# A hybrid decoder step on one core: the attention projection as Strassen products, input forms split at their due times, and the second projection's first units by token halves

## The chip, the cores and the metric

The kernel runs on one core of one Trainium2 chip. The metric is device time in microseconds. An engine is named by its short name: PE is TensorE (matmul), PEld its weight loads, DVE is VectorE, ACT is ScalarE, POOL is GpSimd, SP is SyncE, which issues nearly all transfers here.

## The reference

One layer of a decoder trunk, in float32, for a prompt of 2048 tokens of width 1024 and for 8 single-token samples. What matters for this change:

```python
h = _rmsnorm(x, norm_g) * (1.0 + scale) + shift
z = h @ w_in                                   # 1024 x 6656
q, k, v, ga, xr, gr, ma, mr = jnp.split(z, offs, axis=-1)
...
ya = o * jax.nn.silu(ga)                       # o: attention in a window of 128
xc, conv_new = _causal_conv(xr, conv_buf, w_conv, b_conv)
hs, h_last = _rglru(xc, h0, w_ra, b_ra, w_rx, b_rx, lam)
yr = hs * jax.nn.silu(gr)
merged = jax.nn.sigmoid(ma) * (ya @ w_pa) + jax.nn.sigmoid(mr) * (yr @ w_pr)
y = x + gate * (merged @ w_out)
```

## The kernel before

**Halves and slots.** The prompt is worked on in two halves of 1024 tokens (`s` = 0 and 1), one after the other; the samples ride with the second half. In each half attention comes first (`phase_kv`, `phase_attn`), then `stages` builds a list `seq` of matmul units in a fixed order: the gates of attention `ga`, the two merge gates `ma` and `mr`, the recurrence's inputs `xr` and `gr` (`rnn`), the attention projection `pa`, the recurrence's projection `pr` and the output `out`. Results pass from stage to stage through scratch tensors in HBM: `yad` is the gated attention output, `yrd` that of the recurrence, `tmad` and `tmd` the tanh of the merge gates, `t1d` the attention term of the merge, `mgd` the merged rows, `hd` the normalised input. Each holds 8 row blocks of 128 channels by 1024 tokens, in two column halves of 512 tokens (`chunk`).

**Exact float32 by three products.** An operand is split into a high part in fp32r (ACT casts it) and a low part (DVE subtracts the high part from the source): `split_to`. A product of two such operands is three matmuls: high by high, high by low, low by high.

**Units.** A `Plain` unit computes one block of 128 output channels for 1024 tokens in four calls of `mm`, one for each pair of a contraction half `h` and a token half `c`. A `Fast` unit computes two such blocks (256 channels) by Winograd's variant of Strassen's scheme: seven products instead of eight, each a call of `mm`, in the order of `PROD`. Its right operands are seven forms of the input: three plain quarters (`x11`, `x21`, `x22`) and four differences (`T1` to `T4`). Its left operands are weight quarters and four sums of them (`s1` to `s4`, on DVE). A call of `mm` in either kind is 12 matmuls of 128 x 512. In Fast the results of two PSUM banks are kept and added by `keep`, `add` and `last`.

**The order of everything else.** `Line` runs through `seq`. At step t it issues `mm` number t, then the events registered for t, in the order of their rank (`EVAC`, `SIDE`, `SPLIT`, `FORM`, `CHAIN`, `LATE`, `STORE`, `LOAD`). All engines keep program order, so an event's step fixes its place in its engine's queue. Weights are loaded 7 steps before their unit (`LOADS`) and split 2 steps before their product (`AHEAD`). The recurrence's elementwise chain (`chain`) starts 12 steps after its pair of units and goes on for 27 more. Loads and stores share the queue of SP (`ld` and `st`).

**The stages around the change.** `seq` starts with 18 steps (`m1`, `mr0`, `ga1`); then come `pair(ga2, ga3)`, and four times `rnn(p)` followed, but for the last, by `pair(ma, mr)`. So `rnn_end` is step 130, and the chain of `rnn(3)` runs on into the projection. `forms_of_h` builds the seven forms of the normalised input at the start of the line: differences on DVE and POOL, and splits in `first`, `second` and `third`, at steps t0, t0 + 1 and from t0 + 2 on, for four k with t0 = -1, 1, 3, 5. `pa` takes 8 Plain units (steps 130 to 162); its operand is the 16 quarters of `yad`, split over 10 steps before `rnn_end`. `pr` takes 8 Plain units (162 to 194), its last two interleaved; its operand is the 16 quarters of `yrd`. `phase_h`, in the first half, normalises and transposes the second half's rows, from `rnn_end + 4` on. Step 0 is the first after attention.

**Rings.** SBUF tiles come from two rings in order of release: 28 tiles of 4 KB a partition (`S`) and 35 of 2 KB (`Tt`). The seven forms of the input fill all 28 `S` tiles, and the last unit that reads a form frees it (`final`).

**The start.** Constants of the recurrence (`c4`, `ba2`, and the transposed states `RT`) are made after the first normalisation and before attention.

Of the kernel before, what the change touches and what calls it, by code (L numbers as in the profile page):

```python
# [21 lines left out]
P = 128  # L22
# [19 lines left out]
def tile_hybrid_step(ctx: ExitStack, tc: tile.TileContext, x_prompt, x_sample, cache_k, cache_v, state_conv,  # L42
# [191 lines left out]
    V.memset(q1, 0.25)  # L234

# [107 lines left out]
    for t in wgr + [hsF, yaF]:  # L343
# [8 lines left out]
                                     for t in ("yad", "tmad", "tmd", "sgd", "yrd", "t1d", "mgd"))  # L352
    Gd = dp.tile([P, D], F32, tag="Gd", name="Gd")
# [57 lines left out]
    def phase_h(line, t0):  # L411

        def group(g, t0):
            xts = []

            def load(i):
                xts.append(S([D]))
                r0 = 1024 + g * 512 + i * P
                ld.dma_start(xts[i], xp[r0:r0 + P, :])

            def turn(f):
                ps = PT()
                for i in range(4):
                    T_.transpose(ps[:, i * P:(i + 1) * P], xts[i][:, f * P:(f + 1) * P], ident)
                line.after(1, EVAC, lambda: h_evac(1, ps, 512, f, g * 512, None))
                if f == KT - 1:
                    free(*xts)

            for i in range(4):
                line.on(t0 + 2 * i, LOAD, lambda i=i: load(i))  # L430
                line.on(t0 + 4 + 2 * i, CHAIN, lambda i=i: rms_rows([xts[i][:, h * 512:(h + 1) * 512] for h in range(2)], P))
# [122 lines left out]
    def phase_attn(s, hT, sa, kT, vt, chunks, line):  # L554
# [250 lines left out]
        prefetch(3)  # L805
        pinned[0] = s == 1
# [8 lines left out]
        for i in range(N + 2):  # L815
# [292 lines left out]
    class Fast:  # L1108
# [3 lines left out]
        def __init__(self, line, F, src, evac, samples=None, base=None, late=False):  # L1112
            self.line, self.F, self.src, self.evac, self.samples = line, F, src, evac, samples
            self.base, self.late, self.early = base, late, 0
# [27 lines left out]
        def place(self, s):  # L1142
# [6 lines left out]
            for i, j in ((0, 0), (1, 0), (0, 1), (1, 1)) if late else ((0, 0), (1, 0), (1, 1), (0, 1)):  # L1149
                line.on(s[0] - (3 if late and j == 1 else LOADS + self.early), LOAD, lambda i=i, j=j: self.load(i, j))  # L1150
# [109 lines left out]
    def stages(s, hT, hT1=None, side=None):  # L1260
# [17 lines left out]
        def forms_of_h(k, t0):  # L1278
# [25 lines left out]
            def second():  # L1304
                split("T1", "x11")
                split("T3", "x12")
                free(x["x11"], x["x12"])

            def third():
                split("T4", "x21")  # L1310
                free(x["x21"])
# [4 lines left out]
            line.on(t0 + 1, FORM, second)  # L1316
            line.on(max(t0 + 2, 3), FORM, third)
# [319 lines left out]
        yax, yrx = xtiles(), xtiles()  # L1637
        quarters = [(4 * h + k, c) for h in range(2) for c in range(2) for k in range(4)]
# [3 lines left out]
        def load_pair_rows(w, c0):  # L1642
            wr = w[:, c0:c0 + P].rearrange("(G gg j d) c -> G gg d j c", G=2, gg=2, j=4)

            def load(t, h):
                for gg in range(2):
                    ld.dma_start(t[gg * 64:gg * 64 + 64], wr[h, gg])
            return load

        def pa(f):  # L1650
            tm = {}

            def load(c):
                tm[c] = Tt([512])
                ld.dma_start(tm[c], chunk(tmad, f, c))

            def evac(c, ps):
                V.scalar_tensor_tensor(tm[c], tm[c], 1.0, ps, op0=ALU.add, op1=ALU.mult)
                line.after(1, STORE, lambda: store(c))

            def store(c):
                st.dma_start(chunk(t1d, f, c), tm[c])
                free(tm[c])

            z, d = zS[:, f:f + 1, :], maS[:, f:f + 1, :]
            u = Plain(line, yax, load_pair_rows(w_proj_attn[0], f * P), evac,
                      sample(yaF, z, lambda: V.scalar_tensor_tensor(d, d, 1.0, z, op0=ALU.add, op1=ALU.mult)))
            t0 = len(seq)
            seq.extend((u, n) for n in range(4))
            for c in range(2):  # L1670
                line.on(t0 + c, LOAD, lambda c=c: load(c))
            return u

        for f in range(KT):
            u = pa(f)
        u.gone = set(u.order)
        pa_end = len(seq)
        for i, (k, c) in enumerate(quarters):
            load_split(yrd, yrx, k, c, pa_end - 8 + i // 2 if i < 8 else pa_end - 3 + (i - 8) // 2, 3)

        def pr(f):
# [21 lines left out]
            def done():  # L1703
# [4 lines left out]
                      ((0, 0), (1, 0), (0, 1), (1, 1)) if f >= KT - 2 else Plain.ORDER)  # L1708
            t0 = len(seq)
            if f < KT - 2:  # L1710
                seq.extend((u, n) for n in range(4))
            for c in range(2):
                line.on(t0 + (c - 1 if f < KT - 2 else 4 * c + f - KT), LOAD, lambda c=c: load(c))
            return u

        for f in range(KT):
            last_pr, u = u, pr(f)
        u.gone = set(u.order)
# [118 lines left out]
        if s == 0:  # L1837
# [6 lines left out]
            phase_h(line, rnn_end + 4)  # L1844
# [73 lines left out]
    def state_out():  # L1918
# [11 lines left out]
        free(co)  # L1930
        yield
# [128 lines left out]
    for f in range(KT + 2):  # L2060
# [24 lines left out]
        if f == 4:  # L2085
# [13 lines left out]
    ba2 = C([P, 16], tag="ba2")  # L2099
    V.tensor_scalar(ba2, VT[:, 72:88], 0.5, None, op0=ALU.mult)  # L2100

# [11 lines left out]

    lam = VT[:, 88:96]
    e8, s8, q8, r8 = (M([8]) for _ in range(4))
    A.activation(e8, lam, AF.Abs)
    A.activation(e8, e8, AF.Exp, scale=-1.0)
    V.tensor_scalar(s8, e8, 2.0, None, op0=ALU.add)
    V.reciprocal(s8, s8)
    V.tensor_tensor(s8, s8, e8, op=ALU.mult)  # L2120
    V.tensor_tensor(q8, s8, s8, op=ALU.mult)
    V.tensor_scalar(r8, q8, 1.0 / 17, 1.0 / 15, op0=ALU.mult, op1=ALU.add)
    for n in (13, 11, 9, 7, 5, 3, 1):
        V.tensor_tensor(r8, r8, q8, op=ALU.mult)
        V.tensor_scalar(r8, r8, 1.0 / n, None, op0=ALU.add)
    V.tensor_tensor(r8, r8, s8, op=ALU.mult)
    V.tensor_scalar(s8, lam, -1.0, 0.0, op0=ALU.mult, op1=ALU.max)
    c4 = C([P, 16], tag="c4")
    V.scalar_tensor_tensor(c4[:, 0:8], r8, 2.0, s8, op0=ALU.mult, op1=ALU.add)
    V.tensor_scalar(c4[:, 0:8], c4[:, 0:8], 4.0, None, op0=ALU.mult)  # L2130
    V.tensor_scalar(c4[:, 8:16], c4[:, 0:8], -1.0, None, op0=ALU.mult)


    rows = S([D])
    ld.dma_start(rows[0:24], state_conv[0].rearrange("b r d -> (b r) d"))
    ld.dma_start(rows[24:32], state_h[0])
    ps = PT()
    for k in range(KT):
        T_.transpose(ps[:, k * 32:(k + 1) * 32], rows[0:32, k * P:(k + 1) * P], ident[0:32, 0:32])
    RT = C([P, KT, 32], tag="RT")  # L2140
    V.tensor_copy(RT, ps[:, 0:256].rearrange("p (k c) -> p k c", c=32))
    free(rows)

    hT1, side = [], {}
    line = stages(0, hT, hT1, side)
    attn = phase_attn(0, hT, None, kT, vt, chunks, line)
# [38 lines left out]
```

## Time and profile before

| | |
|---|---|
| median of 3 runs | 1958.66 us (1957.88 to 1959.34) |
| the profiled execution | 1961.09 us, its span 1959.4 us |
| PE, PEld | busy 1915.1 us and 1568.8 us |
| DVE, ACT, POOL | busy 1376.9, 984.5 and 392.3 us |
| matmuls | 11504 |
| transfers | 286.61 MB |

All rows of the profile carry line 60, the helper that records every operation, so groups are told apart by tiles: `pg`, `pq` and `pt` are PSUM pools, `S`, `B`, `H` and `M` are SBUF rings and pools. Matmuls overlap in the pipeline, so the mean of single records is longer than the time from one to the next; the latter counts. A form like `128*128 128x512` is the loaded weight tile and the moving operand.

### The profile page before, as it was taken

The numbers are of one execution on the slowest core, as the hardware profiler recorded it, in microseconds if no ns is written. First come the engines' busy times: TensorE is split into PE (matmuls) and PEld (weight loads), VectorE is DVE, ScalarE is ACT, GpSimd is POOL, SyncE is SP. The second block draws the span as 40 slices with busy tenths as digits, with TensorE's granted clock in tenths as the row PEclk, the third lists the DMA queues.
The fourth block names the chain that finished last, engine by engine and source line by source line (L and its number), as shares of the span: only waits on it lengthen the run. The fifth ranks groups of instructions, "written<-read, shape, count | busy, mean of one in ns | idle before, by whom it ended". The sixth has DMA issues, their size and how long they took to land. (4 is left out here: it accounts for less than half of the span.)

```text
span 1959.4 us, 32369 instructions
## 1 busy us (share of the span) xinstructions
PE 1915.1 (98%) x11504; PEld 1568.8 (80%) x11504; DVE 1376.9 (70%) x2862; ACT 984.5 (50%) x2167; POOL 392.3 (20%) x476
## 2 busy tenths in 40 slices
PE   6899999999999999999999999999999999999999
PEld 4798987778888878887898898777787887777777
DVE  3557778557888876588834777867687879745965
ACT  4445655336675766423423566543575667532321
POOL 3213433000111113060012344400010201111600
PEclk9899999999999999999999999999999999999999
DMA  9521124662433567986721111454233334558673
GB/s 281 176 66 46 53 92 154 180 184 82 142 120 95 164 182 250 327 262 195 231 59 51 47 47 59 152 145 140 87 123 105 120 97 164 149 171 293 216 235 108
DMA packets 307686, 286.61 MB, mean 146 GB/s; under 512 B 57073, under 2 KB 224229, under 8 KB 307486
## 3 DMA queue, kind: packets, MB, share of 16 engines
q1 hardware_dynamic: 307398, 282.41, 45.9%
q0 software_dynamic: 128, 2.15, 0.3%
q8 instruction: 90, 1.47, 0.3%
q14 instruction: 70, 0.57, 0.1%
HBM read 200.69 MB, written 85.93 MB: 146 GB/s over the span
## 5 line engine op out<-in xcount | busy, mean ns | idle before, releaser
L60 PE MATMUL pg<-S,B 128*128 128x512 f32 (+1 forms) x4224 | 1002.1, 392 | 1.5 <-DVE B L60 1.5
L60 PEld LDWEIGHTS pg<-S,B 128*128 128x128 f32 (+1 forms) x4224 | 774.2, 188 | 184.1 <-issue 11.1
L60 DVE TENSOR_TENSOR B<-B,B 128x512 fp32r<-128x512 f32 (+1 forms) x732 | 546.0, 769 | 148.0 <-ACT B L60 137.3
L60 PE MATMUL pq<-S,B 128*128 128x512 f32 (+2 forms) x1920 | 413.1, 379 | 10.0 <-DVE B L60 9.8
L60 PEld LDWEIGHTS pq<-S,B 128*128 128x128 f32 (+1 forms) x1920 | 317.7, 188 | 88.7 <-DVE B L60 14.0
L60 POOL TENSOR_TENSOR B<-B,B 128x512 f32<-128x512 f32 x128 | 191.9, 1516 | 950.6 <-DVE B L60 583.0
L60 ACT CAST B<-B 128x512 fp32r<-128x512 f32 x468 | 279.9, 617 | 114.2 <-DVE B L60 73.7
L60 PE MATMUL pg<-B,S 128*128 128x256 f32 x1872 | 242.8, 285 | 0.0
L60 PEld LDWEIGHTS pg<-B,S 128*128 128x128 f32 x1872 | 227.7, 189 | 10.1 <-issue 9.4
L60 DVE TENSOR_TENSOR S<-B,S 128x512 fp32r<-128x512 f32 x184 | 140.0, 789 | 25.7 <-ACT S L60 25.4
L60 ACT CAST S<-B 128x512 fp32r<-128x512 f32 x184 | 109.1, 621 | 88.5 <-DVE B L60 33.8
L60 ACT ACTIVATE B<-B 128x512 f32<-128x512 f32 (+1 forms) x150 | 93.2, 630 | 118.8 <-DVE B L60 110.4
L60 ACT ACTIVATE B<-B,M 128x129 f32<-128x129 f32 x260 | 102.7, 396 | 91.7 <-DVE M L60 87.5
L60 DVE SCALAR_TENSOR_TENSOR B<-B,pg 128x512 f32<-128x512 f32 x78 | 53.2, 683 | 73.8 <-PE pg L60 58.8
L60 ACT COPY H<-pt 128x256 f32<-128x256 f32 (+1 forms) x55 | 18.5, 337 | 160.6 <-PE pt L60 160.6
L60 DVE TENSOR_TENSOR B<-pq,B 128x512 f32<-128x512 f32 x96 | 66.0, 687 | 43.8 <-PE pq L60 37.9
L60 ACT COPY B<-pg 128x512 f32<-128x512 f32 x80 | 46.8, 585 | 93.0 <-PE pg L60 84.8
L60 POOL TENSOR_TENSOR B<-B,M 128x512 f32<-128x512 f32 x64 | 67.0, 1068 | 104.7 <-DVE M L60 104.7
L60 POOL TENSOR_TENSOR M<-M,mhalf 128x8 f32<-128x8 f32 (+4 forms) x70 | 84.2, 1203 | 5.8
L60 ACT ACTIVATE B<-pg 128x512 f32<-128x512 f32 x76 | 45.2, 595 | 79.8 <-PE pg L60 78.7
L60 DVE SCALAR_TENSOR_TENSOR B<-B,VT,B 128x512 f32<-128x512 f32 x96 | 81.2, 846 | 2.3
L60 DVE SCALAR_TENSOR_TENSOR B<-B,B 128x512 f32<-128x512 f32 x106 | 72.1, 685 | 0.6 <-ACT B L60 0.3
(201 smaller groups left out, 1685.8 us busy)
## 6 DMA issues: line engine op xcount, KB each, us to landing
B<-in_w_in_dram SPq DMA_DIRECT2D x144, 256.0 KB
B<-in_w_in_dram SPq DMA_DIRECT2D x128, 128.0 KB
B<-yad SPq DMA_DIRECT2D x56, 256.0 KB
B<-hd SPq DMA_DIRECT2D x48, 256.0 KB
B<-in_w_out_dram SPq DMA_DIRECT2D x48, 256.0 KB
S<-in_w_ada_dram SPq DMA_DIRECT2D x32, 256.0 KB
S<-in_x_prompt_dram SPq DMA_DIRECT2D x16, 512.0 KB
hd<-B SPq DMA_DIRECT2D x32, 256.0 KB
```

The costliest lines, as they stand in the source:

```text
L60: ins = fn(*args, **kw)
```

## The change

**Attention's projection** becomes four Fast units in two interleaved pairs: 28 steps in place of 32 in each half. Its operand is the seven forms of `yad`. The four differences of each k are taken on POOL (`differences`), from quarters loaded back from `yad`, and stored in a new scratch tensor `yfd`, at steps given by hand; `form_y` loads each of the 28 forms and splits it, from `rnn_end - 9` to `rnn_end + 10`. One `(tanh + 1)` factor in four is applied by DVE with the product, as before; for the other three ACT adds 1 (`plus`) and POOL multiplies. These units load their weights 5 steps ahead.

**The order before it:** the recurrences come first, each followed by a pair, with `ga2` and `ga3` in the first two: `rnn(0)`, `pair(ga2, mr1)`, `rnn(1)`, `pair(ga3, mr2)`, `rnn(2)`, `pair(ma1, mr3)`, `rnn(3)`, `pair(ma2, ma3)`. `rnn_end` stays step 130.

**The input forms** T1, T3 and T4 are split at steps 5 to 8, 7 to 10 and 10 to 13. **`pr`** starts with two units interleaved by token halves, and its operand's quarters come token half 0 first. **`phase_h`** loads rows in halves into the other ring, starts 14 steps later and sets its two groups 9 steps apart. **The recurrence's constants** become `rnn_constants`: loads after attention's first prefetch, the rest in attention's first step. Small ones: the load of the small vectors one step later at the start, `sample_attn`'s last step at 66, `state_out` at `pa_end`.

```diff
@@ phase_h
-                xts.append(S([D]))
+                xts.append([Tt([512]) for _ in range(2)])
...
-            group(g, t0 + 12 * g)
+            group(g, t0 + 9 * g)
@@ phase_attn
         prefetch(3)
+        next(aside, None)
...
+            for _ in aside:
+                pass
             if i != N:
                 slot(3)
@@ forms_of_h
-            line.on(t0 + 1, FORM, second)
-            line.on(max(t0 + 2, 3), FORM, third)
+            for n, src, t in (("T1", "x11", 5), ("T3", "x12", 7), ("T4", "x21", 10)):
+                line.on(t + k, FORM, lambda n=n, src=src: last(n, src))
@@ the order
-        pair(attn_gate(2), attn_gate(3))
-        for p in range(4):
+        ma = [merge(OFF_MA, p, tmad, maS) for p in range(1, 4)]
+        mr = [merge(OFF_MR, p, tmd, mrS) for p in range(1, 4)]
+        ga_end = []
+        for p, ab in enumerate(((attn_gate(2), mr[0]), (attn_gate(3), mr[1]), (ma[0], mr[2]), (ma[1], ma[2]))):
             end = rnn(p)
-            if p < 3:
-                pair(merge(OFF_MA, p + 1, tmad, maS), merge(OFF_MR, p + 1, tmd, mrS))
+            pair(*ab)
+            ga_end.append(len(seq))
@@ the operand of pa
-        for i, (k, c) in enumerate(quarters):
-            load_split(yad, yax, k, c, rnn_end - 11 + 10 * i // 16, 3)
+        def differences(k, t):
...
+            def sub(a, b, o, n):
+                G_.tensor_tensor(x[o], x[a], x[b], op=ALU.subtract)
+                line.after(2, STORE, lambda: st.dma_start(yfd[s, n, k], x[o]))
...
+            line.on(t, LOAD, load)
+            line.on(t + 4, FORM, first)
+            line.on(t + 6, FORM, second)
+            line.on(t + 9, EVAC, lambda: free(*x.values()))
+        for k in range(4):
+            differences(k, ga_end[k // 2] + (12, 41, 26, 39)[k])
+        def form_y(n, k, t):
...
+            line.on(t - 3, LOAD, load)
+            line.on(t, FORM, split)
+        for i, (n, k) in enumerate([(n, k) for _, n, _ in PROD for k in range(4)]):
+            form_y(n, k, rnn_end - 9 + 18 * i // 25)
@@ pa
+            def plus(i, j):
+                A.activation(tm[i, j], tm[i, j], AF.Identity, bias=onec)
+            def evac(i, j, x, t):
+                y = tm[i, j]
+                if t is None:
+                    V.scalar_tensor_tensor(y, y, 1.0, x, op0=ALU.add, op1=ALU.mult)
+                else:
+                    G_.tensor_tensor(y, y, x, op=ALU.mult)
+                    free(t)
+                line.after(1 if t is None else 2, STORE, lambda: store(i, j))
...
+        for p in range(0, 4, 2):
+            (a, la), (b, lb) = pa(p), pa(p + 1)
+            a.ahead = b.ahead = 5
+            t0 = pair(a, b)
@@ pr
-            load_split(yrd, yrx, k, c, pa_end - 8 + i // 2 if i < 8 else pa_end - 3 + (i - 8) // 2, 3)
+            load_split(yrd, yrx, k, c, pa_end - 9 + 7 * i // 8, 3)
...
+            if f == 1:
+                for n in (0, 2):
+                    seq.extend([(last_pr, n), (last_pr, n + 1), (u, n), (u, n + 1)])
@@ stages, at the end
-            phase_h(line, rnn_end + 4)
+            phase_h(line, rnn_end + 18)
...
-            line.steps(sample_attn(), range(7, 30), SIDE)
-            line.steps(state_out(), [end + 1], SIDE)
+            line.steps(sample_attn(), list(range(7, 27)) + [66], SIDE)
+            line.steps(state_out(), [pa_end], SIDE)
@@ the start
-        if f == 4:
+        if f == 5:
             next(rest)
```

More of the change, by code (lines that the diff above doesn't have):

```diff
@@ L234, in tile_hybrid_step @@
     V.memset(q1, 0.25)
+    onec = C([P, 1], tag="onec")
+    V.memset(onec, 1.0)
     def rstd_of(dst, ss, n, inv):
@@ L1302, in first, with last @@
                 free(x["x22"], x["T2"])
[L1304 to L1311, printed above, removed]
+            def last(n, src):
+                split(n, src)
+                free(x[src])
             line.on(t0 - 4, LOAD, load)
@@ L1650, in pa @@
[L1650 to L1672, printed above, removed]
@@ L2112, in tile_hybrid_step @@
     wk, wv = wkv[0][0] + wkv[1][0], wkv[0][1] + wkv[1][1]
[L2114 to L2142, printed above, removed]
     hT1, side = [], {}
     line = stages(0, hT, hT1, side)
-    attn = phase_attn(0, hT, None, kT, vt, chunks, line)
+    attn = phase_attn(0, hT, None, kT, vt, chunks, line, rnn_constants())
     pend = phase_kv(0, hT, None, kT, vt, wk, wv, list(enumerate(kvp)), range(4, 8), bias_expand(), attn)
```

120 lines of the change are left out of this document (96 added, 24 removed).

## The prediction

> **What bounds the kernel now.** First the page, for the engine that never rests; then the waits of TensorE and its instructions by shape; then the chain of waits, for the length of a group of matmuls; last the timeline and the windows around the places that the diff touches.
>
> ```profile
> span 1959.4 us, 32369 instructions
> PE 1915.1 (98%) x11504; PEld 1568.8 (80%) x11504; DVE 1376.9 (70%) x2862; ACT 984.5 (50%) x2167; POOL 392.3 (20%) x476
> L60 PE MATMUL pg<-S,B 128*128 128x512 f32 x4032 | 974.2, 397 | 1.5 <-DVE B L60 1.5
> L60 PE MATMUL pq<-S,B 128*128 128x512 f32 x1584 | 386.1, 398 | 10.0 <-DVE B L60 9.8
> 1361.48 5.55 PE pq L60 x24
> 1367.03 5.55 PE pg L60 x24
> 1372.58 5.60 PE pq L60 x24
> 1378.19 5.57 PE pg L60 x24
> PE pq L60 <- DVE B L60: 9.8, 7, 3.8
> PE pt L60 <- DVE RT L60: 3.2, 1, 3.2
> PE pt L60 <- DMA S<-in_w_ada_dram: 6.0, 6, 2.5
> PE   6899999999999999999999999999999999999999
> ```
>
> TensorE is busy 98% of the span, and where it stands back to back, from 1361.48 to 1378.19 us, 72 matmuls take 16.71 us, 232 ns each; the 397 ns of a single record overlaps its neighbours. One call of `mm` is 12 matmuls, 2.79 us: I call it a slot. The 4032 + 1584 matmuls of 512 columns are 468 slots, 234 in each half of the prompt: 12 in attention, 222 in the written order. Counting starts in twelves gives every slot a time. TensorE waits for little, so a matmul less is worth its 232 ns wherever DVE, ACT and the loads still keep up. That is the question for the attention projection, which is slots 130 to 162:
>
> ```profile
> 707.90:807.40 99.50, 99.50 (x458) 81.05 (x458) 64.56 (x100) 61.56 (x110) 20.84 (x32) 1.00 0.82 262
> 1668.40:1771.80 103.40, 103.05 (x555) 80.56 (x555) 61.44 (x113) 47.42 (x86) 12.29 (x8) 1.00 0.60 180
> ```
>
> (Windows: length, then busy us of PE, PEld, DVE, ACT, POOL, granted clock, DMA share, GB/s.) DVE has 34.9 us idle in the stage of the first half, 42.0 in the second; the clock is full.
>
> **The change part by part.** *Fewer matmuls.* `pa` goes from 8 Plain units of 4 slots to 4 Fast units of 7: 32 slots become 28, in each half. 2 x 4 x 12 = 96 matmuls x 232 ns = 22.3 us less on the path. Sample matmuls and weight bytes stay as many. The Trainium skill's page "TensorE: Matmul & The Clock Gate", section "Back-to-back issue gap", gives N/2.4 + 2.5 ns, which for 512 columns is an estimate of 216 ns and of 20.7 us for the 96; the rows say 232, and I keep them.
>
> *Stalls that go.*
>
> ```profile
> 83.46 0.44 PE L60 MATMUL pt<-ident,H 128*128 128x128 f32 x2 [3.17 <-DVE RT L60]
> 85.60 0.69 PE L60 MATMUL pt<-ident,H 128*128 128x128 f32 x2 [0.65 <-ACT S L60]
> 334.49 4.64 PE L60 MATMUL pq<-S,B 128*128 128x512 f32 x10 [3.84 <-DVE B L60]
> 1273.94 2.58 PE L60 MATMUL pq<-S,B 128*128 128x512 f32 x10 [0.77 <-DVE B L60]
> 699.29 2.58 PE L60 MATMUL pq<-S,B 128*128 128x512 f32 x10 [0.38 <-DVE B L60]
> 1659.70 2.58 PE L60 MATMUL pq<-S,B 128*128 128x512 f32 x10 [1.49 <-DVE B L60]
> ```
>
> The 3.17 us is the wait for the copy into `RT` among the constants of the recurrence, which move into attention's first step, from 92 us on, where the slices of PE above are all 9. Next late at the old place are the K tiles' chains, with the wait of 0.65 us that follows, so I take 3.2 but it may be 2.5. The 3.84 and 0.77 us are in slot 7: a weight split queues behind the splits of T1, T3 and T4, nine of which stand at slots 0 to 5. They move to slots 5 to 13; 9 x 686 ns = 6.2 us leave the queue ahead of that split, more than either wait. Due times of T1, T3, T4 (slots 10, 12, 16) leave two slots or more. The 0.38 and 1.49 us are at the seam before the projection, which is rebuilt. Together 9.6 us. Moving the load of the small vectors one step later, the rows of `phase_h` in halves and its start 14 slots later, `state_out` and the last step of `sample_attn`: nothing, since no wait of TensorE hangs on them; if the cover goes, the waits for `w_ada` (6 of 1 us) have one more, 1 us.
>
> *DVE's added work.* The price of its instructions, alone and beside POOL:
>
> ```profile
> L60 DVE TENSOR_TENSOR B<-B,B 128x512 fp32r<-128x512 f32 x20 | 13.6, 686 | 9.4 <-ACT B L60 9.4
> L60 DVE SCALAR_TENSOR_TENSOR B<-B,VT,B 128x512 f32<-128x512 f32 x4 | 3.0, 750 | 0.1
> L60 DVE TENSOR_TENSOR_SCAN B<-B,HC,B 128x512 f32<-128x512 f32 x32 | 43.9, 1373 | 0.0
> L60 DVE TENSOR_TENSOR S<-B,S 128x512 fp32r<-128x512 f32 x8 | 12.1, 1508 | 0.0
> L60 DVE TENSOR_TENSOR B<-B,B 128x512 f32<-128x512 f32 x12 | 11.0, 915 | 0.5
> L60 DVE TENSOR_TENSOR B<-B,B 128x512 fp32r<-128x512 f32 x6 | 5.2, 867 | 0.0
> L60 POOL TENSOR_TENSOR B<-B,B 128x512 f32<-128x512 f32 x15 | 23.2, 1574 | 16.2 <-DVE B L60 16.2
> ```
>
> The first two rows are from 409 to 463 us, where POOL is idle; the scan's is of the whole run; the last four are from 842 to 876 us, where POOL runs 15 subtractions. There DVE's 26 two-input instructions take 8 x 822 + 12 x 229 + 6 x 181 ns = 10.4 us more than at 686: 0.70 us for each POOL instruction. It can be 0, when DVE reads PSUM or is idle, and 1.57, when DVE stands through all of POOL's. I take 0.75: the window's value, a little more as DVE is fuller at the seam.
>
> Per half the change adds 12 splits of `yad`'s forms (28 for 16), 12 weight splits (28 for 16) and 16 weight sums: 40 x 0.686 = 27.4 us; evacuations stay 16. POOL gets 16 differences and 12 products more: 28 x 0.75 = 21 us of DVE. That is 48 us against 35 to 42 us idle in the stage and what lies before it, so the place decides. I count DVE by six slots. A Fast unit issues 14 (pa: 15), from two slots before its first slot to one after its last; a chain of the recurrence issues three at 750, three at 686 and a scan, 5.7 us.
>
> Calibration, before, slots 114 to 126 (rows below, first two): 24 Fast, 1 silu, 12 forms and 7.5 us of chains make 32.9 us, with 6 POOL x 0.75 = 37.4, against 12 x 2.79 = 33.5 us of matmul. DVE is 3.9 us behind at the end, and the seam's wait was 0.38 and 1.49 us: about 2.5 us of lag are free, since a split is queued two slots ahead.
>
> ```profile
> 660.70:695.50 34.80, 34.80 (x152) 28.13 (x150) 32.19 (x47) 28.31 (x50) 7.45 (x5) 1.00 0.57 191
> 1616.60:1654.50 37.90, 37.90 (x221) 30.23 (x221) 33.52 (x66) 30.75 (x61) 6.71 (x5) 1.00 0.51 170
> 445.10:463.20 18.10, 18.10 (x79) 14.64 (x78) 15.46 (x30) 9.05 (x17) 0.00 (x0) 1.00 0.14 48
> 1383.60:1404.60 21.00, 21.00 (x148) 16.49 (x146) 17.15 (x33) 10.11 (x20) 0.00 (x0) 1.00 0.12 42
> ```
>
> After, slots 114 to 138: the last recurrence's pair now ends at slot 116, so its chains (21.3 us) run in these slots beside two merges, 24 forms and the first weights of `pa`: 49 Fast and 2 silu, 35.0 us; 24 forms, 16.5; sum 72.8, with 12 POOL 81.8. Matmuls: 24 x 2.79 plus four gate groups of 6 = 72.6. Behind by 9.2, less 2.5 free: 6.7 us of wait in the first half. In the second the samples lengthen the slots (37.9 against 34.8 us in the rows), some 4 us here: 2.7.
>
> After, slots 42 to 48: `ga2` now runs beside the first recurrence's chains, its 6 silu and products meet 15 Fast and 7.0 us of chains: 21.4, with 4 POOL 24.4 us, against 18.1 and 21.0 in the last two rows: waits of 3.8 and 0.9 us. The differences (slots 62 to 119) fall where the count is below the matmuls, or over by less than the free lag: nothing; without that cover 0.75 us each, 24 us over both halves.
>
> *ACT, SP, POOL.* ACT casts once for each split, 621 ns here:
>
> ```profile
> L60 ACT CAST S<-B 128x512 fp32r<-128x512 f32 x184 | 109.1, 621 | 88.5 <-DVE B L60 33.8 <-POOL B L60 22.2 <-DMA B<-yrd 16.4
> SPq L60 <- POOL B L60: 63.2, 31, 3.0
> ```
>
> It is at 28.3 of 34.8 us before the seam and gets 24 form casts and the chains together: about as late as DVE, in the same slots, so not counted twice. SP gets 16 + 12 loads and 16 stores more per half; each of the 28 stores after POOL can hold the loads behind it for the 2.0 us (63.2/31) that such waits last now, 3.0 at most. Weights of `pa` are asked for 5 slots ahead, 3 before their cast, 8.4 us: covered. If two waits of 3 us meet a late load, about 2 us once or twice. `pr`'s first two units need only token half 0 at first, whose eight splits are due nine to three slots before `pa` ends: covered.
>
> **The sum.** -22.3 - 9.6 + (6.7 + 2.7 + 3.8 + 0.9 = 14.1) = -17.8 us on this execution's 1961.1 us, which lies 2.4 us above the median 1958.7: 1941.
>
> **The rivals.** *The seam holds.* If DVE and ACT, as queues with slack from several units, swallow the 14.1 us, only the gains stay: 1958.7 - 31.9 = 1927. For it: DVE is busy 32.19 of 34.80 us before the seam, at a wait of 0.38. Against it: the second half waited 1.49 us there with fewer forms and no chain starting.
>
> *POOL and DVE exclude each other.* Each POOL instruction then costs DVE its 1.57 us. Slots 114 to 150: 96.1 us of DVE + 20 x 1.574 = 127.6 against 36 x 2.79 + 5.6 = 106.0: waits of 19.1 and 15.1 us; slots 42 to 48: 7.1 and 4.2. 45.5 us instead of 14.1: 1972, slower. It decides from about 1.2 us each on, where the 31.9 are eaten. For it: the eight forms at 1508 ns. Against it: the same window's other 18 at 867 to 915. The Trainium skill's page "SBUF — State Buffer", section "Who interferes with whom", states this rule: a DVE instruction with two SBUF inputs and a GpSimd instruction that reads SBUF take one port pair by an exclusive lock, and the loser blocks for the whole instruction. The window bears the contention out, its 0.70 us on average only half of the price.
>
> *The saved slots buy nothing,* since the stage waits for data. Its DMA share is 0.82 in the first half; 12 form loads of 256 KB at 262 GB/s are 12 us more, in 11 us less: 81.6 + 12 over 88.3, 5 us late, and at DVE's side 0.9 to 1.1 us a POOL instruction: together 1950 to 1962. Against it: half of `phase_h`'s transfers leave these slots.
>
> **How the numbers follow.** My forecast, 1933 to 1950: 0.50. Seam holds, 1924 to 1933: 0.25. Saved slots mostly lost, 1950 to 1963: 0.16. Exclusion, above 1963: 0.09. The 8-in-10 range is 1926 to 1955: below it lies part of the second case, above it the fourth and half of the third. A measurement here tells 0.2%, 3.9 us, from nothing: faster is below 1954.7, the first two cases and half of the third, 0.82; same 0.09; slower 0.09.
>
> **What would show it.** 5520 matmuls of 512 columns for 5616. No wait for `RT`; none in slot 7. TensorE waiting for DVE at the seam (slots 126 to 140) 7 us in the first half, 3 in the second, and at slots 44 to 48. DVE's two-input mean above 770 ns. Wrong it is made by a first recurrence that waits longer, by form loads held on SP behind POOL's stores (TensorE or ACT waiting for DMA there), or by ACT being the later of the two at the seam.

## The result and the profile after

| | median us | range | ratio to before |
|---|---|---|---|
| before | 1958.66 | 1957.88 to 1961.68 | |
| after | 1949.13 | 1948.08 to 1951.06 | 0.9942 [0.9931, 0.9953] |

The change gains 9.5 us, half of the forecast 17.8; 1941 was forecast, with 1926 to 1955 as range. The profiled execution of after is the one of 1949.13 us, its median; that of before was 2.4 us above its median, so the spans differ by more (12.0 us) than the medians (9.5). The page of after begins:

```profile
span 1947.4 us, 32802 instructions
PE 1894.1 (97%) x11408; PEld 1546.4 (79%) x11408; DVE 1468.5 (75%) x2939; ACT 1034.3 (53%) x2259; POOL 485.6 (25%) x532
```

TensorE's groups and DVE's two-input groups by shape (count, busy us, mean ns, idle before), TensorE's list of waits (us in total, times, longest), and last, for comparison, the third of these DVE groups in before:

```profile
L60 PE MATMUL pg<-S,B 128*128 128x512 f32 x3648 | 887.8, 397 | 11.8 <-DVE B L60 10.3 <-ACT S L60 1.2 <-DVE S L60 0.2
L60 PE MATMUL pq<-S,B 128*128 128x512 f32 x1872 | 456.7, 397 | 8.0 <-DVE B L60 7.4
...
L60 DVE TENSOR_TENSOR B<-B,B 128x512 fp32r<-128x512 f32 x492 | 385.6, 792 | 104.4 <-ACT B L60 103.3 <-issue 0.3
L60 DVE TENSOR_TENSOR B<-B,B 128x512 f32<-128x512 f32 x296 | 228.7, 777 | 9.2 <-DMA B<-mgd 4.3 <-DMA B<-yad 0.3
L60 DVE TENSOR_TENSOR S<-B,S 128x512 fp32r<-128x512 f32 x208 | 171.9, 847 | 29.5 <-ACT S L60 29.4
...
PE pg L60 <- DVE B L60: 10.3, 10, 2.0
PE pq L60 <- DVE B L60: 7.4, 9, 2.5
...
L60 DVE TENSOR_TENSOR S<-B,S 128x512 fp32r<-128x512 f32 x184 | 140.0, 789 | 25.7 <-ACT S L60 25.4
```

The matmuls of 512 columns are 3648 + 1872 = 5520, 96 fewer, as they should be. The wait for `RT` is gone from the list. What came instead is on the `pg` and `pq` rows: 17.7 us of waiting for DVE in 19 waits, where the page of before had 1.5 on `pg` and its list 9.8 on `pq`. DVE's two-input instructions with both inputs in SBUF are longer in all three groups, 777 to 847 ns for 768 to 789.

Counting starts in twelves again, and taking from each stage TensorE's own work (232 ns for a matmul of 512 columns, others about in proportion), leaves how much longer the stage took than its matmuls; this is called the stage's excess below. Us, before and after:

| stage | first half | second half | change |
|---|---|---|---|
| up to slot 0 of the first half | 36.7, 32.9 | | -3.8 |
| slots 0 to 18 | 8.0, 1.0 | -0.9, -1.9 | -8.0 |
| slots 18 to 120 | 1.1, 5.6 | -7.5, -7.5 | +4.5 |
| slots 120 to 130 | 0.7, 1.0 | 1.9, -0.2 | -1.8 |
| `pa`, first half of its slots | 0.0, 7.3 | -0.4, 3.7 | +11.4 |
| `pa`, the rest | 2.3, 0.1 | -0.1, 0.1 | -2.0 |
| `pr`, first 16 slots | 0.8, 5.6 | -0.7, 1.4 | +6.9 |
| `pr`, the rest, and `out` | 3.3, 4.8 | 0.7, 1.9 | +2.7 |

The second half's attention adds 0.2. With it the column makes +10.1; with 22.2 us less of matmul work that is the span's change, 1947.4 - 1959.4 = -12.0, within rounding. (A negative entry is a stage with many narrow sample matmuls, which cost less than they are counted at. How the narrow ones are counted moves an entry by up to 4 us, a change by under 1 us.)

### The profile page after: what moved, and what is told of

Its sections match the earlier page's. It is cut to its first block, busy times and chain, and to the rows that moved or that the text cites. A ratio compares the mean times of both kernels' runs of the same rounds, so it can differ in the third digit from the quotient of the medians.

```text
span 1947.4 us, 32802 instructions
## 1 busy us (share of the span) xinstructions
PE 1894.1 (97%) x11408; PEld 1546.4 (79%) x11408; DVE 1468.5 (75%) x2939; ACT 1034.3 (53%) x2259; POOL 485.6 (25%) x532
## 4 chain that ended last, share of the span: by engine, by line
PE 46%; DVE 5%; DMA 1%; issue 1%; ACT 1%; SPq 0%; POOL 0%; DVEq 0%; ACTq 0%
PE pg L60 26%; PE pq L60 14%; PE pt L60 6%; DVE B L60 3%; DVE S L60 2%; ACT B L60 1%; DMA B<-mgd 0%; DMA B<-yrd 0%; DMA B<-tmd 0%; ACT S L60 0%; DMA B<-yfd 0%; DMA tmad<-B 0%; SPq L60 0%; DMA mgd<-B 0%; DVE xrS L60 0%
## 5 line engine op out<-in xcount | busy, mean ns | idle before, releaser
L60 PE MATMUL pg<-S,B 128*128 128x512 f32 (+1 forms) x3840 | 915.6, 391 | 11.8 <-DVE B L60 10.3
L60 PEld LDWEIGHTS pg<-S,B 128*128 128x128 f32 (+1 forms) x3840 | 701.2, 188 | 181.5 <-DVE B L60 16.4
L60 DVE TENSOR_TENSOR B<-B,B 128x512 fp32r<-128x512 f32 (+1 forms) x788 | 601.1, 786 | 113.6 <-ACT B L60 103.3
L60 POOL TENSOR_TENSOR B<-B,B 128x512 f32<-128x512 f32 x184 | 286.4, 1570 | 858.9 <-ACT B L60 359.6
L60 PE MATMUL pq<-S,B 128*128 128x512 f32 (+2 forms) x2208 | 483.7, 381 | 8.0 <-DVE B L60 7.4
L60 PEld LDWEIGHTS pq<-S,B 128*128 128x128 f32 (+1 forms) x2208 | 370.8, 188 | 101.6 <-DVE B L60 14.9
L60 ACT CAST B<-B 128x512 fp32r<-128x512 f32 x492 | 295.1, 618 | 129.6 <-DVE B L60 82.4
L60 DVE TENSOR_TENSOR S<-B,S 128x512 fp32r<-128x512 f32 x208 | 171.9, 847 | 29.5 <-ACT S L60 29.4
L60 ACT CAST S<-B 128x512 fp32r<-128x512 f32 x208 | 124.0, 620 | 58.2 <-DVE B L60 18.8
L60 DVE TENSOR_TENSOR B<-pq,B 128x512 f32<-128x512 f32 x112 | 76.6, 684 | 39.1 <-PE pq L60 39.1
L60 ACT COPY H<-pt 128x256 f32<-128x256 f32 (+1 forms) x51 | 17.9, 351 | 132.5 <-PE pt L60 132.5
L60 POOL TENSOR_SCALAR M<-M 128x8 f32<-128x8 f32 (+5 forms) x71 | 15.1, 212 | 255.9 <-DVE M L60 249.2
```

The source lines that it names most:

```text
L60: ins = fn(*args, **kw)
```

## The experiments

All kernels below were timed against before on the same chip; before's median was 1959.83, 1958.83 and 1958.91 us in the three groups.

**The two small parts alone.** Before, with the constants of the recurrence moved (and the load of the small vectors one step later, as in the change) and the forms split when due, nothing else:

```diff
-            line.on(t0 + 1, FORM, second)
-            line.on(max(t0 + 2, 3), FORM, third)
+            for n, src, t in (("T1", "x11", 5), ("T3", "x12", 7), ("T4", "x21", 10)):
+                line.on(t + k, FORM, lambda n=n, src=src: last(n, src))
...
+    def rnn_constants():
```

> The kernel before with two parts of the change alone: the recurrence's constants moved into attention (with the small vectors' load one step later), and the splits of T1, T3, T4 at their due steps. Theory: in the changed kernel's trace these two gave 3.8 us (slot 0 of the first half at 303.6 for 307.3 us) and 8.0 us (slots 0 to 18 of both halves), so alone they give 1958.7 - 11.8 = 1947 us, ratio 0.994, as much as the whole change; the projection by Strassen, with its new order, then adds nothing. Rival: the parts need each other, the earlier start is lost later in the kernel before, and this gives 1951 to 1955.

Measured: 1952.77 us (1948.72 to 1954.04), ratio 0.9961 [0.9948, 0.9973]. The theory's 1947 was missed, and the time lies in the rival's range; but the rival's reason, a gain lost again later, accounts for 0.6 us only. The profiled span is 1950.8, 8.6 us under before's; slots 0 to 18 account for 6.7 in the first half and 1.0 in the second, the start for 1.5. What is short is the start: slot 0 of the first half stands at 305.8 us here and at 303.6 in after, with the same code ahead of it. In the traces of all kernels with that code it stands at 301.5 to 305.8 us (before: 307.3), so the table's 3.8 us for the start is uncertain by about 2. These two parts carry most of the whole gain. Between this kernel and after lies the projection by Strassen's scheme with its new order: 3.4 us by the spans, of which 2.2 lie ahead of slot 0, so 1.2 behind it. The two intervals touch, so by the times alone a net gain of that part is not shown.

**Which engine holds the new projection's first slots.** Three kernels leave out something of the changed kernel's work on `yad`'s forms: in each half 21 of 28 low parts (DVE's), or 21 of 28 casts (ACT's), or all 16 differences (POOL's).

```diff
-                split_to(FY[n][k][:, 0, :], FY[n][k][:, 1, :], box[0])
+                if k == 0:
+                    split_to(FY[n][k][:, 0, :], FY[n][k][:, 1, :], box[0])
+                else:
+                    A.copy(FY[n][k][:, 0, :], box[0])                                      # no_low
+                    V.tensor_tensor(FY[n][k][:, 1, :], box[0], FY[n][0][:, 0, :], ...)     # no_cast
...
-        for k in range(4):
-            differences(k, ga_end[k // 2] + (12, 41, 26, 39)[k])                           # no_differences
```

> The changed kernel, with the low parts of 21 of the 28 forms of the attention output left out in each half (the products use the low part of k = 0 for all four k): DVE has 21 x 0.69 = 14.4 us less around the seam, all else stays. Theory, DVE is the last at the seam: the waits of slots 130 to 144 (7.3 us in the first half, 4.1 in the second) go, and some of those at the start of the recurrence's projection: 1936 to 1940 us. Rival, ACT's casts are the last there: 1946 to 1950.

> The changed kernel, with the casts of 21 of the 28 forms left out in each half (the low parts are taken against the high part of k = 0, and the products use it for all four k): ACT has 21 x 0.62 = 13 us less around the seam, DVE's work stays. Theory, DVE is the last at the seam: 1945 to 1950 us, the same seam waits. Rival, ACT is the last (it is busy 0.82 to 0.92 of slots 120 to 138): the seam's 11 us go, 1936 to 1940.

> The changed kernel without the four differences for each k (the T forms are loaded from the plain quarters instead): 16 POOL subtractions, 16 loads and 16 stores less in each half. Theory, POOL costs DVE 0.75 us an instruction and the differences lie mostly in DVE's free time: the 4 us of waits in slots 46 to 102 go, no more: 1944 to 1948 us. Rival, POOL and DVE exclude each other in full, 1.57 us each, and this lags on: 1933 to 1940.

Measured: without the low parts 1936.79 us (ratio 0.9875 [0.9860, 0.9891]); without the casts 1947.73 (0.9937 [0.9923, 0.9950]); without the differences 1947.26 (0.9935 [0.9922, 0.9949]). The windows from 692 to 754 us of after, without the low parts and without the casts, in that order (length, then busy us of PE, PEld, DVE, ACT, POOL, granted clock, DMA share, GB/s):

```profile
692.00:754.00 62.00, 56.72 (x233) 42.57 (x232) 61.40 (x79) 45.10 (x78) 23.34 (x14) 1.00 0.75 235
```

```profile
692.00:754.00 62.00, 61.46 (x262) 48.51 (x261) 53.30 (x72) 47.53 (x82) 21.67 (x14) 1.00 0.78 252
```

```profile
692.00:754.00 62.00, 57.41 (x239) 43.72 (x238) 61.69 (x80) 37.39 (x62) 24.23 (x14) 1.00 0.76 238
```

After, DVE is busy 61.40 of 62.00 us and TensorE idle for 5.28. With 8 us taken off DVE TensorE's idle time falls to 0.54. With 8 us taken off ACT it stays at 4.59. So DVE's amount of work holds these slots, and the rival of ACT falls. That of the differences falls too: without them the excess of `pa`'s first slots stays (7.7 and 4.1 us). All three times lie in the ranges of their theories.

**The same amount, later.** If the amount counts, work that can wait should be moved out. The last recurrence's second chains can:

```diff
-            c = {(0, 0): t0 + 12, (0, 1): t0 + 15, (1, 0): t0 + 22, (1, 1): t0 + 25}
+            c = {(0, 0): t0 + 12, (0, 1): t0 + 15, (1, 0): t0 + (34 if p == 3 else 22), (1, 1): t0 + (37 if p == 3 else 25)}
```

> The changed kernel with one step later: of the last quarter of the recurrent part, the second 128 features' gates, scan and output (about 11 us of DVE's work in each half) are put 12 slots of 12 matmuls later, out of the slots in which the projection of attention begins. Theory A (at the beginning of that projection DVE has simply more work than time, so any 11 us taken out of it frees TensorE, whatever work it is): TensorE's waits there, 7.3 and 3.7 us, shrink to under 2 us each, as they did when the low parts were left out, and the run is near 1942 us (1939 to 1946). Rival B (the work is only put off: the later slots have products and the next projection's forms of their own, and the waits appear there or at the start of the next projection): the same time, 1948 to 1951. Rival C (what counts is not the amount but the order in DVE's queue): no more than 2 us, and the waits at the first slots stay.

Measured: 1938.48 us (1934.84 to 1940.91), ratio 0.9886 [0.9868, 0.9904]: 10.6 us under the changed kernel. The excess of `pa`'s first slots falls from 7.3 and 3.7 to 0.8 and -1.0 us, the rest of `pa` takes 1.6 and 0.8 of it back. The same window:

```profile
692.00:754.00 62.00, 61.58 (x265) 49.46 (x264) 59.09 (x85) 46.74 (x83) 15.41 (x10) 1.00 0.84 261
```

TensorE idles for 0.42 us here, with the same work in the run as a whole. (Some of POOL's instructions went with the chain, 14 to 10 in this window.) The theory holds; the time lies just under its range, slots 120 to 130 giving another 0.9 and 1.5 us.

**What a POOL product costs DVE.** The twelve products a half that the change gave to POOL, done by DVE in one instruction each:

```diff
-                if t is None:
-                    V.scalar_tensor_tensor(y, y, 1.0, x, op0=ALU.add, op1=ALU.mult)
-                else:
-                    G_.tensor_tensor(y, y, x, op=ALU.mult)
-                    free(t)
+                V.scalar_tensor_tensor(y, y, 1.0, x, op0=ALU.add, op1=ALU.mult)
...
-                        line.on(t0 + 2 * n, LATE, lambda i=i, j=j: plus(i, j))
```

> The changed kernel with the three products of each unit of attention's projection that GpSimd does (with ScalarE's addition before each) done by DVE in one instruction each, as one of the four is already. Some 24 products a half leave GpSimd for DVE: 24 x 0.686 = 16.5 us more on DVE. Theory A (each GpSimd product of two inputs costs DVE 0.7 to 0.9 us by lengthening the DVE operations beside it, so the product costs DVE about the same wherever it is done): the waits in the first slots stay within 3 us, DVE's two-input mean falls to near 700 ns there, the wait for GpSimd's queue at the start of the other projection (4.8 us over before in the first half) shrinks, and the run is between 1944 and 1949 us. Rival B (the two exclude each other wholly, 1.6 to 1.7 us for each product): DVE gains about 1 us a product in the full slots, some 11 in the first half: near 1937. Rival C (the lengthening is not due to GpSimd but to the accesses of TensorE and the DMAs): DVE has 11 us more in the full slots of each half, and the run is near 1960.

The count in this text is wrong: the 24 products are those of both halves, 12 in each. Measured: 1946.45 us (1942.19 to 1946.72), ratio 0.9923 [0.9906, 0.9940], in theory A's range; the interval overlaps that of after. The best measure of the price is DVE's busy time in the pages of this kernel, of the one without differences and, from the last experiments below, of the late chain alone and of the late chain with the products on DVE:

```profile
PE 1895.2 (97%) x11408; PEld 1549.2 (80%) x11408; DVE 1465.3 (75%) x2963; ACT 1019.9 (52%) x2235; POOL 444.0 (23%) x508
```

```profile
PE 1895.7 (97%) x11408; PEld 1548.5 (80%) x11408; DVE 1442.2 (74%) x2939; ACT 1033.8 (53%) x2259; POOL 436.9 (22%) x500
```

```profile
PE 1889.6 (98%) x11408; PEld 1547.4 (80%) x11408; DVE 1461.4 (76%) x2939; ACT 1036.0 (54%) x2259; POOL 484.3 (25%) x532
```

```profile
PE 1891.5 (98%) x11408; PEld 1548.7 (80%) x11408; DVE 1455.3 (75%) x2963; ACT 1022.3 (53%) x2235; POOL 441.6 (23%) x508
```

With DVE's own instructions the same in number (2939), 32 POOL differences fewer take 1468.5 - 1442.2 = 26.3 us off DVE: 0.82 us each. With 24 products moved onto DVE, it has 24 instructions more and is busy 3.2 us less: 0.686 + 0.13 = 0.82 us each. (The kernel with the later stores, below, has the same DVE instructions as after and is busy 1462.7 us, 5.8 less. So 26.3 us are clear of what order alone does, 3.2 are not.) The price of 1.57 us for every POOL instruction, which would make 50 us of the 26.3, falls, and so does the view that POOL costs DVE nothing. Giving a product to POOL where DVE is full therefore gains nothing that shows here: DVE loses about 0.82 us for the 0.69 saved. The groups of DVE and POOL in after between 705.7 and 753.3 us show it at the place:

```profile
L60 DVE TENSOR_TENSOR S<-B,S 128x512 fp32r<-128x512 f32 x18 | 17.3, 985 | 0.0
L60 DVE TENSOR_TENSOR B<-B,B 128x512 fp32r<-128x512 f32 x16 | 14.0, 872 | 0.3 <-issue 0.3
L60 DVE TENSOR_TENSOR B<-B,B 128x512 f32<-128x512 f32 x9 | 7.7, 861 | 0.1
...
L60 POOL TENSOR_TENSOR B<-B,B 128x512 f32<-128x512 f32 x11 | 18.9, 1728 | 30.0 <-ACT B L60 12.6 <-DVE HC L60 11.5 <-issue 4.5
```

Against 686 ns, the 43 instructions lose 18 x 0.299 + 16 x 0.186 + 9 x 0.175 = 9.9 us beside 11 POOL products, 0.90 each. With the products on DVE the first row's mean is 806 ns in this window. The Trainium skill's page "SBUF — State Buffer", section "Who interferes with whom", has the loser of the shared port pair blocked for the whole instruction. The trace agrees, one instruction at a time. After's DVE has 997 TENSOR_TENSOR instructions of 128x512 with both inputs in SBUF: the 803 that no POOL instruction of this size overlaps take 684 ns on average and 717 at most; of the 176 that one of POOL's `B<-B,B` overlaps, 79 take more than 1.6 us, the longest 1.83. At the seam the two engines take turns (timelines of DVE and POOL in after):

```profile
729.09 1.79 DVE L60 TENSOR_TENSOR B<-B,B 128x512 fp32r<-128x512 f32 x1
730.80 1.78 DVE L60 TENSOR_TENSOR S<-B,S 128x512 fp32r<-128x512 f32 x1
...
728.88 3.15 POOL L60 TENSOR_TENSOR B<-B,B 128x512 f32<-128x512 f32 x2 [0.87 <-ACT B L60]
```

So a DVE instruction can stand for 1.1 us. POOL's own take 1.29 us where no such DVE instruction is beside them (six in after) and up to 1.8 elsewhere: the 1.57 us contains POOL's waits for DVE. And not every POOL instruction meets a DVE instruction that it can hold. So single instructions do exclude each other, and 0.82 us is the average price here.

**The stores of the states.** In after, the second half's first slots of `pr` wait for a chain of three: SP issues eleven small stores, then a load of `yrd`; ACT waits for that load; TensorE waits for ACT (timelines of SP, ACT and PE; in brackets the idle time and what ended it):

```profile
1760.94 5.19 SPq L60 DMA_DIRECT2D out_dram<-B  x11
...
1770.26 0.62 ACT L60 CAST S<-B 128x512 fp32r<-128x512 f32 x1 [8.19 <-DMA B<-yrd]
1774.45 0.62 ACT L60 CAST S<-B 128x512 fp32r<-128x512 f32 x1 [3.57 <-DMA B<-yrd]
...
1775.12 0.49 PE L60 MATMUL pg<-S,B 128*128 128x512 f32 x1 [1.25 <-ACT S L60]
```

```diff
-            line.steps(state_out(), [pa_end], SIDE)
+            line.steps(state_out(), [pa_end + 16], SIDE)
```

> The changed kernel with the small stores of the second half's states put 16 slots later on the queue that issues the loads, behind the loads of the other projection's inputs rather than ahead of them. Theory A (these stores, 5.2 us on the queue, hold back the loads for which ScalarE and then TensorE wait at the start of the other projection in the second half, 2.1 us longer than before): about 2 us faster, 1947 (1945.5 to 1948.5). Rival B (the loads wait for a free buffer or for DVE, the stores stand beside that): within 1 us of the changed kernel, 1949. Rival C (the stores at their new place hold back the loads of the weights behind them): 1951 or more.

Measured: 1947.39 us (1945.69 to 1952.43), ratio 0.9937 [0.9918, 0.9957], which by itself does not tell the kernel from after. The trace does: that stage's excess falls from 1.4 to -0.8 us, and the wait is gone:

```profile
1766.40 11.38 PE L60 MATMUL pg<-S,B 128*128 128x512 f32 x48
```

Half is given back at the stage's end (0.3 to 1.3 us). The stores did hold the loads.

**Together.** The late chain with the products on DVE, and the same with the later stores:

> The later chain and the products on DVE together. Theory A (DVE's work in the first slots is what counts; a product costs DVE 0.7 to 0.9 us on GpSimd and 0.69 on DVE itself): like the later chain alone, 1942, or 1 to 3 us better because nothing waits any more behind GpSimd's products (1938 to 1943). Rival B (wholly exclusive): 1932 to 1936. Rival C (GpSimd's products cost DVE nothing): 10 us or more slower than the later chain alone, since the 12 slots freed are filled again.

> Later chain, products on DVE and the later stores of the states together: the run with the first two took 1932.7 us. Theory A (the stores of the states hold back loads for which TensorE waits at the start of the second half's other projection): another 1 to 2 us, 1931 (1929 to 1932.5). Rival B (with the chain later and no product queued behind GpSimd, that start has no wait left, its excess over TensorE's own work being -0.9 us already): the same, 1932.7 within 1 us. Rival C (the stores now meet the loads behind them): 1934 or more.

Measured: 1932.71 us (1931.95 to 1933.32; ratio 0.9859 [0.9843, 0.9876]) and 1932.72 (1930.27 to 1937.09; 0.9866 [0.9853, 0.9880]). The first is better than its theory, 5.8 us under the late chain alone, in the range that the exclusive rival gave; yet that rival's price is not there: DVE's busy time fell by 1461.4 - 1455.3 = 6.1 us with 24 instructions more, 0.94 us a product and not 1.57. The gain is at the start of `pr`, 5.4 to 2.7 us of excess in the first half and 0.9 to -0.9 in the second, and in the rest of `pa`, 1.6 to 0.1 and 0.9 to 0.2; `pa`'s first slots give back about 1 us. That this was work queued behind POOL's products fits, and is shown for the start of `pr` alone, further down. With that wait gone the stores cost nothing any more, so there the rival holds.

The last wait of over 1 us for DVE in the first half stood at the start of `out`. PE's timeline of the kernel of all three, and the groups of DVE and POOL between 830 and 872 us:

```profile
870.39 4.83 PE L60 MATMUL pg<-S,B 128*128 128x512 f32 x13 [1.85 <-DVE B L60]
...
L60 DVE TENSOR_TENSOR S<-B,S 128x512 fp32r<-128x512 f32 x11 | 13.2, 1207 | 2.2 <-ACT S L60 2.2
L60 DVE TENSOR_TENSOR B<-B,B 128x512 f32<-128x512 f32 x12 | 11.5, 955 | 0.5
...
L60 POOL TENSOR_TENSOR B<-B,B 128x512 f32<-128x512 f32 x18 | 28.5, 1610 | 14.2 <-DVE B L60 14.2
```

The same pairing as at the seam, in code that the change never touched: in `forms_of_out`,

```diff
-                sub(G_, "x22", "x12", "x12")
+                sub(V, "x22", "x12", "x12")
...
-                sub(G_, "x21", "T2", "x21")
+                sub(V, "x21", "T2", "x21")
```

> The same as the kernel of all three, with the two subtractions of GpSimd per set of forms of the output projection (8 in each half, beside 16 of its multiplications) done by DVE. In the run with later chain and products on DVE, 18 GpSimd operations of 1.6 us lie in the 42 us ahead of the output projection, DVE's operations there take 0.95 to 1.2 us against 0.68, and TensorE waits 1.9 us for DVE at the output's start in each half. Theory A (a GpSimd operation takes DVE at least as long as doing it): the wait at the output's start goes from 2.0 to about 1 us in the first half and 1.8 to 1 in the second, and the whole is 1 to 3 us less than the kernel of all three. Rival B (the forms are late because of their loads and buffers): no change within 1 us. Rival C (DVE there has no room for 8 x 0.69 us more): 2 us or more slower.

Measured: 1927.84 us (1926.21 to 1933.57), ratio 0.9843 [0.9828, 0.9858]; the intervals of the two still touch. The gain of 4.9 us is more than theory A's 1 to 3. Of the spans' difference, 5.0 us, 3.7 are in the second 16 slots of `pr` in the first half and 1.3 in the second half's `out`. About 1.7 of the 3.7 us come by the clock: in the kernel of all three the wait of 1.85 us is followed by 3.41 us at a granted clock of 0.50 (871.48 to 874.89 us), and here the wait and that stretch are both missing. Between the same two times the groups are now:

```profile
L60 DVE TENSOR_TENSOR B<-B,B 128x512 f32<-128x512 f32 x21 | 17.4, 828 | 1.1
L60 DVE TENSOR_TENSOR S<-B,S 128x512 fp32r<-128x512 f32 x14 | 13.1, 951 | 0.6 <-ACT S L60 0.6
...
L60 POOL TENSOR_TENSOR B<-B,B 128x512 f32<-128x512 f32 x11 | 18.0, 1666 | 11.0 <-DVE S L60 6.0 <-PE pg L60 5.0
```

Its list of waits has 3.0 us for DVE on `pg` and `pq`, of after's 17.7:

```profile
PE pg L60 <- DVE B L60: 1.8, 5, 0.5
PE pq L60 <- DVE B L60: 1.2, 2, 0.8
```

That is 31.1 us under before's median in its group and 21.3 under after's, which was timed in another group.

## Why the prediction was partly right

| step | forecast | measured |
|---|---|---|
| 96 matmuls fewer | -22.3 | -22.2 (at 232 ns each) |
| stalls at the start and in slot 7 | -7.8 | -11.8 |
| slots 18 to 120 | +4.7 | +4.5, at other places |
| seam, less its old stalls | +9.4 - 1.9 = +7.5 | +7.6 |
| `pr` and `out` | 0 | +9.6 |
| sum | -17.9 | -12.1 (with 0.2 of attention) |

The sign came out as worked out, and so did the matmuls: the last 14 slots of `pa`, which nothing disturbs, take 39.1 us in the first half, 2.79 each. The seam's mechanism came out too. Its count by six slots, DVE's work against 2.79 us a slot, gave 6.7 and 2.7 us; 7.3 and 3.7 were found in the stage, and the waits stand one behind the other as a queue that never catches up (PE's timeline of after, idle time in brackets):

```profile
696.31 2.58 PE L60 MATMUL pq<-S,B 128*128 128x512 f32 x10 [0.73 <-DVE B L60]
...
707.45 2.60 PE L60 MATMUL pg<-S,B 128*128 128x512 f32 x10 [1.15 <-DVE B L60]
...
712.93 2.59 PE L60 MATMUL pg<-S,B 128*128 128x512 f32 x10 [0.41 <-DVE B L60]
...
747.98 11.07 PE L60 MATMUL pg<-S,B 128*128 128x512 f32 x46 [1.53 <-DVE B L60]
```

The price of 0.75 us a POOL instruction was nearly right (0.82 over the run, 0.90 at the seam).

That the seam's row agrees to 0.1 us is luck: `pa`'s first slots became 11.4 us longer against 9.4 counted, and the rest of `pa` gave back 2.0 that nobody had counted. The row of slots 18 to 120 is luck as well, as shown below.

**The step that failed** is "nothing" for what was moved past queues: the sentences that `phase_h` 14 slots later and `state_out` cost nothing, and that `pr`'s first units are covered. Against that nothing stand 6.9 us at `pr`'s start, and 2.7 behind it. In the second half the stores of `state_out` stand ahead of `yrd`'s loads, as shown. In the first half TensorE waits 2.02 us for DVE at 797.94 us; ahead of it, in the timelines of DVE, ACT and POOL:

```profile
795.81 0.88 DVE L60 TENSOR_SCALAR B<-B,M 128x512 f32<-128x512 f32 x2 [0.72 <-POOL M L60]
...
793.98 0.62 ACT L60 CAST B<-B 128x512 fp32r<-128x512 f32 x1 [2.92 <-POOL B L60]
...
792.34 1.60 POOL L60 TENSOR_TENSOR B<-B,B 128x512 f32<-128x512 f32 x1 [1.29 <-DVE B L60]
```

The row scaling of `phase_h` on DVE waits for a small POOL result that is queued behind POOL's product, and ACT's cast for a tile that POOL still holds. With the products on DVE that stage's excess falls from 5.6 to 3.1 us and this wait disappears, so POOL's products account for 2.5 of its 4.8 us. Whether moving `phase_h` back would do as much, or free the remainder, was not tried. Of the 3.1 us and of the 2.7 behind `pr`'s start the cause is shown only as far as the last experiment goes (3.7 us by `out`'s subtractions, the clock included).

**Two smaller terms.** Slots 42 to 48 were given 3.8 and 0.9 us of wait; the profile shows one of 0.45 us there (PE's timeline):

```profile
454.95 2.60 PE L60 MATMUL pg<-S,B 128*128 128x512 f32 x10 [0.45 <-DVE B L60]
```

One part of the count was wrong there: the new order puts six more gate matmuls into these slots, so TensorE has 19.5 us of work in the first half, not the 18.1 of before. The excess of the stage is in slots 46 to 120 of the first half, 4.6 us at three places (slots 47 to 49, 74 to 77 and 104), in four waits of 0.43 to 0.53 us for DVE and what follows them. DVE is busy for 98 or 99% at all three (windows of after, figures as above):

```profile
437.00:457.40 20.40, 19.95 (x86) 15.62 (x85) 20.00 (x28) 15.22 (x26) 7.81 (x5) 1.00 0.36 124
534.60:549.00 14.40, 13.30 (x54) 9.57 (x53) 14.29 (x22) 11.28 (x19) 2.23 (x2) 1.00 0.38 126
622.00:633.00 11.00, 10.54 (x46) 8.27 (x46) 10.90 (x12) 7.96 (x14) 5.64 (x5) 1.00 0.32 121
```

So DVE's work was the cause that was forecast, at places that the count had not given. Without the differences two of the four waits and 1.5 of the 4.6 us go: that is what the price of "nothing" for these missed. And slot 7's stall was worth more than its 3.84 us: the whole stage fell by 7.0, because the prediction priced a wait at its length and left out the clock, as told below.

**The rivals.** "The seam holds" fell at the seam itself. "POOL and DVE exclude each other" fell by its price of 1.57 us for each POOL instruction, not by its mechanism: single instructions do exclude each other. "The saved slots buy nothing" gave 1950 to 1962 and came within a microsecond in size: taken alone, the Strassen part bought 3.4 us by the spans, 1.2 of them behind slot 0. Its cause was another, not the transfers but DVE's amount of work, and 12 slots' delay of one chain got 10.6 us of it back.

## What to carry to other kernels

When fewer matmuls mean more elementwise work ahead of them, count the elementwise engine slot by slot, and in the same change put later whatever can wait: here one moved chain was worth more than the change of scheme had gained by itself. In a kernel like this one, offload a two-input operation to POOL only where DVE has idle time; where DVE was full, it paid for the product all the same. A step moved past a queue has no price of nothing: list what it issues and who stands behind it, stores included. And price a wait of TensorE with the clock that follows it: 3.84 us cost 7.0 here.

## What the hardware showed that was not expected

A wait of TensorE can cost nearly twice its length. In before, 3.84 us of waiting in slot 7 and 3.17 for `RT` each led into a stretch at half clock (windows of before; the seventh figure, after POOL's, is the granted clock):

```profile
83.40:91.40 8.00, 7.29 (x31) 5.85 (x32) 4.94 (x23) 3.01 (x10) 2.48 (x3) 0.57 0.00 1
334.40:341.00 6.60, 6.51 (x16) 5.18 (x17) 6.44 (x12) 2.44 (x5) 0.00 (x0) 0.53 0.52 191
```

The 16 matmuls of the second row run at 0.53 for 6.6 us: 3.1 us lost beside the wait, which with the 3.84 makes the 7.0 that the stage fell by. The Trainium skill's page "TensorE: Matmul & The Clock Gate", section "Why this matters for your kernels", asks for no idle gap above about 3 us for this reason, and the two rows agree. Shorter ones did it too: after's wait of 2.45 us at 1864.84 us was followed by 4 us at 0.61, and one of 2.24 us with the products on DVE, at 1704.91, by 4 us at 0.57; but one of 2.28 us in the same run, at 746.65, and one of 2.67 us with the late chain left the clock at 1.00. So length alone does not decide.

The clock records of the traces show what does. In each trace all stretches at half clock start on one grid of 3.41 us (in before at 53.85, 84.58 and 333.75 us, 9 and 73 steps apart), and in mid-run they last one or two steps. Of the steps at full clock in the twelve traces, from 70 us on, all nine in which TensorE idles for 54% or more are followed by half clock, none in which it idles for less than 50%, and 6 of the 13 between. So one wait can cost more in one run than in another. After and the kernel with the later stores have the same code at the start of `pr` in the first half, and there the same wait of 2.02 us, which ends at 797.94 us in the one and at 797.30 in the other (windows along each trace's grid, after first):

```profile
793.63:797.04 3.41, 2.29 (x10) 1.50 (x8) 2.69 (x5) 3.03 (x8) 2.35 (x6) 1.00 0.84 273
797.04:800.45 3.41, 2.51 (x11) 2.02 (x12) 3.41 (x7) 0.49 (x1) 0.56 (x2) 1.00 0.80 266
...
794.08:797.49 3.41, 1.39 (x7) 0.81 (x6) 2.69 (x6) 2.77 (x7) 1.90 (x5) 1.00 0.71 241
797.49:800.90 3.41, 3.41 (x9) 2.63 (x9) 3.41 (x7) 0.00 (x0) 0.00 (x0) 0.50 0.81 264
```

In after the wait is spread over two steps and the clock stays full; in the other it falls into one step, and the next runs at 0.50. Such a step loses about 1.7 us. Differences of this size between single traces, also in the tables above, can be the clock's and not the kernel's.
